# GLA gate logits of a hybrid encoder layer: both products first, ScalarE moves them out of PSUM, VectorE's clamp moves into a later instruction

## The chip, the cores and the metric

The kernel runs on one NeuronCore of a Trainium2 chip. The metric is the device time of one execution in microseconds (us). The core's engines work side by side, each through its own instruction list in order: TensorE (PE in the profile), VectorE (DVE), ScalarE (ACT), GpSimd (POOL) and SyncE (SP), which here only issues DMAs. They meet at semaphores: an instruction that needs another engine's result waits, and everything behind it on its engine waits too.

## What is computed

One layer of a streaming encoder over 2048 prompt tokens and 32 sample tokens, model width 1024. After an RMSNorm one projection feeds a sliding-window attention and a gated linear attention (GLA, 4 heads with 64-wide keys and 128-wide values). Both outputs go through `w_out`, then a feed-forward with squared ReLU. The change lies in GLA's forget gate:

```python
log_a = jax.nn.log_sigmoid((ca @ w_alpha + b_alpha)) / GLA_TAU      # 16 -> 256 columns, TAU = 16
def step(S, inp):                                                   # gla_chunked, one chunk
    qc, kc, vc, gc = inp
    b = jnp.cumsum(gc, axis=1)
    o_inter = jnp.einsum('blhk,bhkv->blhv', qc * jnp.exp(b), S)
    ... # o_intra: q.k products weighted with exp(b_t - b_s), causal, times v
    S_new = jnp.exp(bL)[..., None] * S + jnp.einsum('bshk,bshv->bhkv', kc * jnp.exp(bL - b), vc)
```

The kernel computes `log_sigmoid(x)` as `min(x, 0) - ln(1 + exp(-|x|))`, and its running sum over the tokens of a 128-token tile.

## The kernel before

The program has three phases: attention (to about 395 us), GLA with the start of `w_out` (to about 810 us), and the feed-forward, which fills the rest with dense matmuls. Matrix products split each fp32 operand into a high and a low part and add three products.

The GLA phase goes through eight pairs of token tiles, called halves 0 to 7 in the code (half 0 also has the 32 sample tokens). For each half `project` computes q (`zq`, two products), k (`zk`, two) and v (`zv`, one for each tile). VectorE scales q and k out of PSUM into the tile `kq` (L721). For each token tile a generator `gla_tile` then runs these steps:

- GpSimd forms differences of `cc`, the running sum of the log gate (tiles `E`, L790 and L798); ScalarE takes Abs and Exp of them (L800, L113); VectorE multiplies them with k and q (L805, L809).
- TensorE computes the blocks `A` of the token-by-token matrix (104 small matmuls, into two PSUM tiles A0 and A1). VectorE copies them with masks into the buffer AT (L863, L869, L874), and the diagonal from `dk` (L821). TensorE transposes the decayed keys into `dk`; ScalarE moves them to `kdT`.
- TensorE computes the outputs `go` and the state update; VectorE updates the state `Sp` (L906); ScalarE squares `go` (into the second half of the tile `v`, L912); VectorE sums the squares (`ssg`, L913), takes an inverse root by small instructions (L170 to L175), and scales into `g` (L918). Later TensorE transposes `g` (`gTp`), ScalarE copies it (`gT`, L927), and SyncE stores it.

The forget gate of the next half is computed by the generator `decay`. It loads `ca`, multiplies it with `wal` (two products of 128 columns, the tile name `la`), and from that makes `la` and `cc`. In halves 1 to 7 both products lie in one PSUM tile, `one_bank`. With each product ScalarE takes the absolute value with the bias (L649), and VectorE takes the clamped value with the bias (L650). Then ScalarE takes Exp and Ln (L113, each with a table load before it), VectorE subtracts (L655) and takes the running sum by two scans (L657). `tail` is `gates`, which applies Silu to the output gate tiles `g` on ScalarE; GpSimd then multiplies them with a constant (L702).

The order of TensorE's list is fixed by the order in which the Python code issues matmuls. The order on the other engines is set by the scheduler of the tile framework, which works with its own estimates and with priorities. The framework adds the waits: a matmul that writes to a PSUM tile waits for the earlier readers of that tile, and two engines that read one PSUM tile do so one after the other. The PSUM pool `pss` has five tiles, which `la`, `dk`, `A0`, `A1`, `gTp` and `go` share; `psm` has three, for `zq`, `zk` and `zv`.

Of the kernel before, what the change touches and what calls it, by code (L numbers as in the profile page):

```python
# [12 lines left out]
AF = mybir.ActivationFunctionType  # L13
ALU = mybir.AluOpType
# [5 lines left out]
P = 128  # L20
# [8 lines left out]
class Builder:  # L29
# [600 lines left out]
    def decay(self, h, tail=None):  # L630

        V, S, Q = self.V, self.S, self.Q
        _, d0, wal, bal, one, _ = self.gla_consts
        tiles = self.halves[h]
        N = sum(self.rows(t) for t in tiles)
        resets = d0 if h == 0 else d0[:, NS:]
        tmp = self.io_tile(f"la_{h}")
        la, ca = tmp[:, :576].rearrange("p (q t) -> p q t", q=2), tmp[:16, 576:864]
        off = 0
        for t in tiles:  # L640
            Q.dma_start(ca[:, off : off + self.rows(t)], self.cad[t])
            off += self.rows(t)
        yield 5000 + 4000 * (h == 0)
        cc = self.cc[h] = self.mid.tile([P, 2, 288], F32, tag="cc", name=f"cc_{h}")
        one_bank = N <= 2 * P and self.ps_s(f"la_{h}")
        for p in range(2):
            ps = one_bank[:, p * N : (p + 1) * N] if one_bank else self.ps_s(f"la_{h}_{p}")[:, :N]
            self.mm(ps, wal[:, p * P : (p + 1) * P], ca[:, :N], True, True)
            S.activation(la[:, p, :N], ps, AF.Abs, bias=bal[:, p : p + 1])  # L649
            V.tensor_scalar(out=cc[:, p, :N], in0=ps, scalar1=bal[:, p : p + 1], scalar2=0.0, op0=ALU.add, op1=ALU.min)  # L650
        self.table(la[:, :, :N], la[:, :, :N], AF.Exp, scale=-1.0)
        self.table(la[:, :, :N], la[:, :, :N], AF.Ln, bias=one)
        if tail:
            tail(h)
        V.tensor_tensor(out=la[:, :, :N], in0=cc[:, :, :N], in1=la[:, :, :N], op=ALU.subtract)  # L655
        for p in range(2):
            V.tensor_tensor_scan(  # L657
                out=cc[:, p, :N], data0=resets, data1=la[:, p, :N], initial=0.0, op0=ALU.mult, op1=ALU.add
            )

    def gla_phase(self):
        tc, a, V, S, G, Q = self.tc, self.a, self.V, self.S, self.G, self.Q
        nt = self.nt
        with ExitStack() as ctx:
# [3 lines left out]
            masks, d0, wal, bal, one, ones = self.gla_consts  # L668
# [16 lines left out]
            vs, gs, vready, glas, stage, decs = {}, {}, set(), [], {}, {0: self.dec0}  # L685

            def reach(n, s):

                while n >= 0 and stage[n] < s:
                    self.clock = max(self.clock, glas[n][0])  # L690
                    self._resume(glas[n])
# [12 lines left out]
            def project(h):  # L704
                tiles = halves[h]
                (nh, nl), N, rb = self.gla_toks.pop(h)
                rh, rl = (lambda kb: nh[:, kb, :N]), (lambda kb: nl[:, kb, :N])

                kq = wk.tile([P, 4 * 288], F32, tag="kq", name=f"kq_{h}")
                offs = np.cumsum([0] + [self.rows(t) for t in tiles])  # L710
                runs = [(0, 1, NS)] * (len(tiles) == 3) + [(N - 2 * P, 2, P)]
                for wt, x, sc, nm in ((self.wqg, 1, 0.125, "q"), (self.wkg, 0, 1.0, "k")):
                    for p in range(2):
                        if h == 0 and self.head0:
                            ps = self.head0.pop(0)
                        else:
                            ps = self.gla_cols(wt, p, f"z{nm}_{h}_{p}", rh, rl, N)
                        for at, j, L in runs:
                            dst = kq[:, 4 * at : 4 * (at + j * L)].rearrange("q (j x p t) -> q x p j t", j=j, x=2, p=2)[:, x, p]
                            src, rbs = (y[:, at : at + j * L].rearrange("q (j t) -> q j t", j=j) for y in (ps, rb))  # L720
                            V.scalar_tensor_tensor(out=dst, in0=src, scalar=sc, in1=rbs, op0=ALU.mult, op1=ALU.mult)  # L721
                wvg = self.wvg
                if h == len(halves) - 1:
                    self.prepare_ffn(1)
                    self.prepare_ffn(0)
                self.finish(decs[h])
                for i, t in enumerate(tiles):
                    r = self.rows(t)
                    if i < 2:
                        n = len(glas)  # L730
                        reach(n - 2, 2)
                        glas.append(None)
                        glas[n] = self.spawn(gla_tile(n, t, int(offs[i]), kq, self.cc[h]), 0 if i else 0)
                        self.tick()
                    ts = slice(int(offs[i]), int(offs[i]) + r)
                    ps = self.ps_m(f"zv_{t}")[:r]
                    self.gemm_wide(ps, lambda kb: nh[:, kb, ts], lambda kb: nl[:, kb, ts], wvg)
                    reach(len(vs) - 3, 3)
                    vs[t] = self.io_tile(f"v_{t}")
                    S.activation(vs[t][:r, :512], ps, AF.Copy, scale=self.rstd[:r, t : t + 1])  # L740
                    vready.add(t)
                    if h == len(halves) - 1 and i == len(tiles) - 1:
                        self.prepare_ffn(2)
                    if i == 2:
                        n = len(glas)
                        reach(n - 2, 2)
                        glas.append(None)
                        glas[n] = self.spawn(gla_tile(n, t, int(offs[i]), kq, self.cc[h]), 0)
                        self.tick()
                    if i == len(tiles) - 2 and h + 1 < len(halves):  # L750
                        decs[h + 1] = self.spawn(self.decay(h + 1, gates), 1500)
# [13 lines left out]
            def gla_tile(n, t, off, kq, cc):  # L765
                stage[n] = 0
                L = self.rows(t)
# [3 lines left out]
                kq, cv = kq[:, 4 * off : 4 * (off + L)].rearrange("q (x p t) -> q x p t", x=2, p=2), cc[:, :, tk]  # L771
                k, q = kq[:, 0], kq[:, 1]
# [1 line left out]
                NL = len(lv)  # L774
                first = key == "p" and t == 0
                qk = wk.tile([P, 2, P], F32, tag="qkp", name=f"qkp_{t}")
                (G if 0 else V).tensor_tensor(out=qk[:, :, :L], in0=q, in1=k, op=ALU.mult)
                ec = wk.tile([P, 2, P], F32, tag="ec", name=f"ec_{t}", bufs=3)
                self.table(ec[:, :, :L], cv, AF.Exp, scale=1.0 / 16)
                if not first:  # L780
                    Qc = wk.tile([P, 2, P], F32, tag="Qc", name=f"Qc_{t}", bufs=3)
                    (G if 0 else V).tensor_tensor(out=Qc[:, :, :L], in0=q, in1=ec[:, :, :L], op=ALU.mult)
                Es = []
                for gi, g_ in enumerate([list(range(0, 4)), list(range(4, NL + 1))]):
                    E = wk.tile([P, 4, 2 * P], F32, tag="E", name=f"E_{t}_{gi}", bufs=4)
                    E = E[:, :, : 2 * L].rearrange("q s (p t) -> q s p t", p=2)
                    for s_, li in enumerate(g_):
                        ev = E[:, s_]
                        if li == NL:
                            G.tensor_tensor(  # L790
                                out=ev, in0=cv[:, :, L - 1 : L].broadcast_to([P, 2, L]), in1=cv, op=ALU.subtract
# [23 lines left out]
                ps = self.ps_s(f"dk_{t}")  # L815
# [12 lines left out]
                def K(li):  # L828
                    return Es[0][:, li] if li < 4 else Es[1][:, li - 4]
# [12 lines left out]
                for li, m in enumerate(lv):  # L842
# [3 lines left out]
                    for p in range(2):  # L846
                        for a0 in range(nh if m < 64 else 1):
                            s0, s1 = (slice(0, 64), slice(64, P)) if m == 64 else (slice(a0 * 64, a0 * 64 + L // nh),) * 2
                            for hh in range(2):
                                x = K(li)[hh * 64 : hh * 64 + 64, p]  # L850
# [8 lines left out]
                for li, m in enumerate(lv):  # L859
                    for hh in range(2):  # L860
                        src = at[li][hh]
# [3 lines left out]
                        for a0 in range(nh):  # L865
# [6 lines left out]
                            dst = A4[r, :, hh, r].rearrange("s p (n h m) -> s p n h m", h=2, m=m)[:, :, :, 1, :]  # L872
# [15 lines left out]
                ps = [self.ps_s(f"go{hh}_{t}") for hh in range(2)]  # L888
# [525 lines left out]
```

## Time and profile before

| | us |
|---|---|
| three runs | 2373.58, 2368.15, 2366.94 (median 2368.15) |
| the profiled execution | 2377.03 (span 2375.2) |
| TensorE busy in the span | 2270.3 |
| VectorE busy | 1454.0 |
| GpSimd busy | 1161.2 |
| ScalarE busy | 950.0 |

Times in rows are counted from the first instruction of the span. A row of the timeline gives start, duration, engine, line, operation, output and inputs, how many instructions are merged in it, and in brackets how long the engine was idle before it and what ended that. A row of the waits gives total, number and longest. A row of the windows gives, for a stretch, its length, the busy time and number of instructions of PE, PEld (weight loads), DVE, ACT and POOL, then the granted TensorE clock as a share of full speed, and the DMA share and rate. In the chain of work that ended last, a row gives start, duration and what worked.

### The profile page before, as it was taken

Reading aid. Unit: us, or ns where it says so; the run is one execution under the profiler, and the core shown is the slowest. Engines: PE = TensorE matmul, PEld = TensorE weight load, DVE = VectorE, ACT = ScalarE, POOL = GpSimd, SP = SyncE. Lnnn points to the kernel's source line nnn. Section 1 sums busy time; section 2 is a strip of 40 time slices with the busy share of each in tenths; the row PEclk is TensorE's granted clock in tenths of the full one; section 3 lists DMA queues with packets and bytes.
Section 4 is the critical chain, followed back from the end, with each engine's and each line's share of the span. In section 5 each row is a group of like instructions: output and inputs, shape, how many; then the busy total and the mean of one; then the engine's idle time right before and its main releaser. Section 6 shows DMA issues by size and latency. Waiting matters only on the chain.

```text
span 2375.2 us, 39804 instructions
## 1 busy us (share of the span) xinstructions
PE 2270.3 (96%) x15389; PEld 2128.0 (90%) x15389; DVE 1454.0 (61%) x3686; ACT 950.0 (40%) x1945; POOL 1161.2 (49%) x956
## 2 busy tenths in 40 slices
PE   6999999899887899999999899999999999999999
PEld 5777776688776899999999899999999999999999
DVE  6666656688778755555564755555556655555555
ACT  3554444454452633333334533333334533333331
POOL 3221224232241457766754466666663546666662
PEclk8999999889898999999999999999999999999999
DMA  8864564322322422232226222222227122222211
GB/s 205 157 127 101 129 164 121 85 73 59 101 82 74 120 80 72 77 102 72 71 84 194 80 72 71 72 71 72 72 61 222 36 80 72 72 71 72 72 63 51
DMA packets 214461, 221.56 MB, mean 93 GB/s; under 512 B 38736, under 2 KB 178976, under 8 KB 214272
## 3 DMA queue, kind: packets, MB, share of 16 engines
q1 hardware_dynamic: 214272, 219.02, 32.9%
q8 instruction: 121, 1.98, 0.3%
q14 instruction: 68, 0.56, 0.1%
HBM read 180.08 MB, written 38.91 MB: 92 GB/s over the span
## 4 chain that ended last, share of the span: by engine, by line
PE 85%; DVE 8%; DMA 3%; ACT 1%; POOL 1%; issue 1%; SPq 0%; ACTq 0%; DVEq 0%; POOLq 0%
PE dn L105 30%; PE op L105 7%; PE zq L105 5%; PE PS4B L105 4%; PE PA11B L105 4%; PE PA12B L105 4%; PE PS2T L105 3%; PE PS1T L105 3%; PE PA22T L105 3%; PE PS3T L105 3%; PE zr L105 3%; PE zv L105 3%; PE zkv L105 2%; PE go L105 2%; PE zk L105 2%; PE O L105 1%
## 5 line engine op out<-in xcount | busy, mean ns | idle before, releaser
L1082 POOL TENSOR_TENSOR wu<-stage,wu 128x512 fp32r<-128x512 f32 x336 | 435.4, 1305 | 525.0 <-ACT wu L1081 525.0
L1249 DVE TENSOR_TENSOR y<-y,dn 128x360 f32<-128x360 f32 (+1 forms) x768 | 392.6, 515 | 219.6 <-PE dn L105 216.7
L1081 ACT ACTIVATE wu<-stage 128x512 fp32r<-128x512 f32 x336 | 206.0, 627 | 488.6 <-PE dn L105 224.7
L1084 POOL TENSOR_TENSOR stage<-stage 128x512 f32<-128x512 f32 x192 | 250.7, 1306 | 7.5
L1202 ACT ACTIVATE r<-PA11B 128x360 f32<-128x360 f32 (+1 forms) x48 | 22.1, 460 | 315.6 <-PE PA11B L105 315.6
L1189 DVE TENSOR_TENSOR PA12B<-PA12B,r 128x360 f32<-128x360 f32 (+1 forms) x48 | 25.3, 527 | 150.2 <-PE PA12B L105 150.2
L702 POOL TENSOR_TENSOR g<-g,ggla 128x512 f32<-128x512 f32 (+1 forms) x17 | 22.2, 1330 | 194.2 <-ACT g L113 194.2
L105 PE MATMUL PS2T<-T2h,wu 128*128 128x360 f32 (+1 forms) x384 | 100.5, 324 | 13.4 <-ACT T2h L1114 13.4
L105 PE MATMUL PA22T<-T4h,wu 128*128 128x360 f32 (+1 forms) x384 | 102.7, 331 | 0.0
L105 PE MATMUL PS4B<-B22h,wu 128*128 128x360 f32 (+1 forms) x384 | 101.5, 328 | 0.0
L105 PE MATMUL PS3T<-T3h,wu 128*128 128x360 f32 (+1 forms) x384 | 99.7, 323 | 0.0
L105 PE MATMUL PS1T<-T1h,wu 128*128 128x360 f32 (+1 forms) x384 | 98.8, 321 | 0.0
L105 PE MATMUL PA11B<-B11h,wu 128*128 128x360 f32 (+1 forms) x384 | 98.8, 321 | 0.0
L105 PE MATMUL PA12B<-B21h,wu 128*128 128x360 f32 (+1 forms) x384 | 98.7, 321 | 0.0
L874 DVE COPY_PREDICATED AT<-masks,A 64x64 f32<-64x64 int32 (+1 forms) x330 | 82.8, 253 | 13.4 <-PE A L105 3.5
L105 PEld LDWEIGHTS PS2T<-T2h,wu 128*128 128x128 f32 x384 | 68.8, 190 | 14.2 <-ACT T2h L1114 14.2
L798 POOL TENSOR_TENSOR E<-cc 128x256 f32<-128x256 f32 (+1 forms) x117 | 68.3, 619 | 17.8 <-PE A L105 17.8
L497 ACT ACTIVATE P<-S,negm 128x192 f32<-128x192 f32 (+2 forms) x128 | 51.6, 417 | 51.7 <-DVE negm L492 34.9
L105 PEld LDWEIGHTS PA22T<-T4h,wu 128*128 128x128 f32 x384 | 71.2, 196 | 0.0
L105 PEld LDWEIGHTS PS4B<-B22h,wu 128*128 128x128 f32 x384 | 70.1, 193 | 0.0
L105 PEld LDWEIGHTS PS3T<-T3h,wu 128*128 128x128 f32 x384 | 69.1, 190 | 0.0
L105 PEld LDWEIGHTS PS1T<-T1h,wu 128*128 128x128 f32 x384 | 68.1, 188 | 0.0
(1006 smaller groups left out, 7766.4 us busy)
## 6 DMA issues: line engine op xcount, KB each, us to landing
stage<-in_w_up SPq DMA_DIRECT2D x96, 512.0 KB, 3.8
stage<-in_w_down SPq DMA_DIRECT2D x96, 512.0 KB, 3.8
stage<-in_w_out SPq DMA_DIRECT2D x24, 512.0 KB, 4.7
xT1a<-in_xT_prompt SPq DMA_DIRECT2D x16, 512.0 KB, 8.8
stage<-in_w_in SPq DMA_DIRECT2D x16, 512.0 KB, 5.0
x1a<-in_x_prompt SPq DMA_DIRECT2D x16, 512.0 KB, 6.6
out_yT_prompt<-y SPq DMA_DIRECT2D x32, 180.0 KB, 3.0
m<-mixT SPq DMA_DIRECT2D x11, 512.0 KB, 3.9
```

The costliest lines, as they stand in the source:

```text
L105: self._pe(self.T.matmul(out, lhsT, rhs, start=start, stop=stop), ns)
L497: S.activation(Pt[:, u, :n], sp[:, jp], AF.Exp, bias=negm[:, ch, u : u + 1], scale=0.125, accum_out=rsum[:, ch, u : u + 1],)
L702: G.tensor_tensor(out=gv, in0=gv, in1=ggla[:r].unsqueeze(1).broadcast_to([r, 4, P]), op=ALU.mult)
L798: G.tensor_tensor(out=e4, in0=c4, in1=ref, op=ALU.subtract)
L874: V.copy_predicated(dst, mk.unsqueeze(1).broadcast_to([L // nh, 2, w // m, m]), src[r].rearrange("s p (n m) -> s p n m", m=m),)
L1081: S.activation(h, src, AF.Copy)
L1082: G.tensor_tensor(out=l, in0=src, in1=f32(h), op=ALU.subtract)
L1084: tt = lambda o, x, y, op: G.tensor_tensor(out=o, in0=x, in1=y, op=op)
L1189: tt = lambda out, x, y, op=ALU.add: V.tensor_tensor(out=out, in0=x, in1=y, op=op)
L1202: S.activation(r0, product(b, "A11", "B11"), AF.Copy)
L1249: V.tensor_tensor(out=yg[:, f, :], in0=yg[:, f, :], in1=ps, op=ALU.add)
```

## The change

In `decay` both matmuls are issued before anything reads them. ScalarE then moves each product out with its bias (Identity, into `cc`), and takes the absolute value of both at once from `cc` in SBUF. VectorE no longer reads the PSUM tile. Its clamp `min(x, 0)` becomes the first operation of the subtraction, now a scalar_tensor_tensor. In `project` the scaling of q and k gets a higher scheduling priority. Two other edits of the diff (a choice that was always VectorE, a delay that was always 0) change nothing.

```diff
@@ decay @@
-        one_bank = N <= 2 * P and self.ps_s(f"la_{h}")
+        if N <= 2 * P:
+            x = self.ps_s(f"la_{h}")
+            ps = [x[:, p * N : (p + 1) * N] for p in range(2)]
+        else:
+            ps = [self.ps_s(f"la_{h}_{p}")[:, :N] for p in range(2)]
         for p in range(2):
-            ps = one_bank[:, p * N : (p + 1) * N] if one_bank else self.ps_s(f"la_{h}_{p}")[:, :N]
-            self.mm(ps, wal[:, p * P : (p + 1) * P], ca[:, :N], True, True)
-            S.activation(la[:, p, :N], ps, AF.Abs, bias=bal[:, p : p + 1])
-            V.tensor_scalar(out=cc[:, p, :N], in0=ps, scalar1=bal[:, p : p + 1], scalar2=0.0, op0=ALU.add, op1=ALU.min)
+            self.mm(ps[p], wal[:, p * P : (p + 1) * P], ca[:, :N], True, True)
+        for p in range(2):
+            S.activation(cc[:, p, :N], ps[p], AF.Identity, bias=bal[:, p : p + 1])
+        S.activation(la[:, :, :N], cc[:, :, :N], AF.Abs)
         self.table(la[:, :, :N], la[:, :, :N], AF.Exp, scale=-1.0)
         self.table(la[:, :, :N], la[:, :, :N], AF.Ln, bias=one)
         if tail:
             tail(h)
-        V.tensor_tensor(out=la[:, :, :N], in0=cc[:, :, :N], in1=la[:, :, :N], op=ALU.subtract)
+        V.scalar_tensor_tensor(
+            out=la[:, :, :N], in0=cc[:, :, :N], scalar=0.0, in1=la[:, :, :N], op0=ALU.min, op1=ALU.subtract
+        )
@@ project @@
-                            V.scalar_tensor_tensor(out=dst, in0=src, scalar=sc, in1=rbs, op0=ALU.mult, op1=ALU.mult)
+                            with tc.high_priority(500):
+                                V.scalar_tensor_tensor(out=dst, in0=src, scalar=sc, in1=rbs, op0=ALU.mult, op1=ALU.mult)
```

The lists of TensorE and GpSimd keep their order, instruction for instruction. SyncE's list differs at one place (one load of `w_out` now stands behind the load of `g_15` and the store of `gT_10`). VectorE's and ScalarE's lists change around each `decay`. Half 3 stands for halves 3 to 6; numbers at the end of a name tell buffers apart.

VectorE, half 3, from the last masked copies of A of token tile 4 to the first use of the new `cc`; before:

```order
L874 COPY_PREDICATED AT1_4493<-masks_2828,A0_4_5856 64x2x32 x2
L874 COPY_PREDICATED AT1_4493<-masks_2828,A1_4_5857 64x2x32 x2
L650 TENSOR_SCALAR cc_3_5936<-la_3_5937,packed_177 128x256
L821 COPY_PREDICATED AT0_4492<-packed_177,dk_5_5965 128x512
L655 TENSOR_TENSOR la_3_5803<-cc_3_5936,la_3_5803 128x2x256
L657 SCALAR_TENSOR_TENSOR cc_3_5936<-d0_2829,la_3_5803 128x256 x2
L721 SCALAR_TENSOR_TENSOR kq_3_5838<-zq_3_0_5839,rb_3_5265 128x2x128
L721 SCALAR_TENSOR_TENSOR kq_3_5838<-zq_3_1_5984,rb_3_5265 128x2x128
L782 TENSOR_TENSOR Qc_6_6196<-kq_3_5838,ec_6_6194 128x256
```

and in the changed kernel:

```order
L881 COPY_PREDICATED AT1_4492<-masks_2828,A0_4_5853 64x2x32 x2
L881 COPY_PREDICATED AT1_4492<-masks_2828,A1_4_5854 64x2x32 x2
L659 SCALAR_TENSOR_TENSOR la_3_5800<-cc_3_5933,la_3_5800 128x2x256
L728 SCALAR_TENSOR_TENSOR kq_3_5835<-zq_3_0_5836,rb_3_5263 128x2x128
L663 SCALAR_TENSOR_TENSOR cc_3_5933<-d0_2829,la_3_5800 128x256 x2
L728 SCALAR_TENSOR_TENSOR kq_3_5835<-zq_3_1_5980,rb_3_5263 128x2x128
L789 TENSOR_TENSOR Qc_6_6192<-kq_3_5835,ec_6_6190 128x256
```

The two clamps are gone (the other stood among the masked copies of A), the copy from `dk_5` has moved in among the masked copies, and the first scaling of q has moved ahead of the scans.

ScalarE, half 3, from the move of `kdT_4` to Silu of the gate tiles; before:

```order
L836 ACTIVATE kdT_4_5854<-dk_4_5806 128x256
L649 ACTIVATE la_3_5803<-la_3_5937,packed_177 128x256 x2
L113 ACTIVATE la_3_5803<-la_3_5803 128x2x256
L927 ACTIVATE gT_2_5955<-gTp_2_5950 128x512
L113 ACT_TABLE_LOAD
L113 ACTIVATE la_3_5803<-la_3_5803,one_2831 128x2x256
L113 ACT_TABLE_LOAD
L113 ACTIVATE g_6_5946<-g_6_5946 128x512
```

and in the changed kernel:

```order
L843 ACTIVATE kdT_4_5851<-dk_4_5803 128x256
L653 ACTIVATE cc_3_5933<-la_3_5934,packed_177 128x256 x2
L934 ACTIVATE gT_2_5951<-gTp_2_5946 128x512
L654 ACTIVATE la_3_5800<-cc_3_5933 128x2x256
L113 ACTIVATE la_3_5800<-la_3_5800 128x2x256
L113 ACT_TABLE_LOAD
L113 ACTIVATE la_3_5800<-la_3_5800,one_2831 128x2x256
L113 ACT_TABLE_LOAD
L113 ACTIVATE g_6_5942<-g_6_5942 128x512
```

There is one Abs of 512 columns more, and the copy `gT_2` now stands ahead of Abs and Exp. The number of table loads is the same.

ScalarE, half 7, around the squares of token tile 12; before:

```order
L800 ACTIVATE E_15_0_8400<-E_15_0_8400 128x1024
L912 ACTIVATE v_12_7843<-go0_12_8192 128x256
L800 ACTIVATE E_15_1_8411<-E_15_1_8411 128x1024
L912 ACTIVATE v_12_7843<-go1_12_8193 128x256
L113 ACTIVATE ec_15_8396<-cc_7_8007 128x256
```

and in the changed kernel:

```order
L807 ACTIVATE E_15_0_8392<-E_15_0_8392 128x1024
L919 ACTIVATE v_12_7836<-go0_12_8184 128x256
L919 ACTIVATE v_12_7836<-go1_12_8185 128x256
L113 ACTIVATE ec_15_8388<-cc_7_8000 128x256
L113 ACTIVATE E_15_0_8392<-E_15_0_8392 128x1024
```

Abs of `E_15_1` no longer stands between the two squares; its Exp has moved behind two casts of `w_out` weights.

More of the change, by code (lines that the diff above doesn't have):

```diff
@@ L732, in project @@
                         glas.append(None)
-                        glas[n] = self.spawn(gla_tile(n, t, int(offs[i]), kq, self.cc[h]), 0 if i else 0)
+                        glas[n] = self.spawn(gla_tile(n, t, int(offs[i]), kq, self.cc[h]))
                         self.tick()
@@ L776, in gla_tile @@
                 qk = wk.tile([P, 2, P], F32, tag="qkp", name=f"qkp_{t}")
-                (G if 0 else V).tensor_tensor(out=qk[:, :, :L], in0=q, in1=k, op=ALU.mult)
+                V.tensor_tensor(out=qk[:, :, :L], in0=q, in1=k, op=ALU.mult)
                 ec = wk.tile([P, 2, P], F32, tag="ec", name=f"ec_{t}", bufs=3)
@@ L781, in gla_tile @@
                     Qc = wk.tile([P, 2, P], F32, tag="Qc", name=f"Qc_{t}", bufs=3)
-                    (G if 0 else V).tensor_tensor(out=Qc[:, :, :L], in0=q, in1=ec[:, :, :L], op=ALU.mult)
+                    V.tensor_tensor(out=Qc[:, :, :L], in0=q, in1=ec[:, :, :L], op=ALU.mult)
                 Es = []
```

## Prediction

> **What bounds the kernel now.** I read the page's engine shares first, then TensorE's waits, then the stretches of the GLA phase, then the rows of one half there.
>
> ```profile
> PE 2270.3 (96%) x15389; PEld 2128.0 (90%) x15389; DVE 1454.0 (61%) x3686; ACT 950.0 (40%) x1945; POOL 1161.2 (49%) x956
> PE la L105 <- DVE cc L650: 20.9, 7, 6.0
> 513.50:555.44 41.94, 39.55 (x439) 33.27 (x433) 34.15 (x121) 20.16 (x29) 12.45 (x18) 0.92 0.30 82
> 517.00:520.00 3.00, 3.00 (x18) 2.10 (x17) 2.69 (x11) 2.28 (x4) 0.00 (x0) 0.50 0.79 173
> 720.00:760.00 40.00, 26.71 (x343) 23.22 (x342) 37.31 (x105) 9.77 (x17) 6.69 (x3) 0.90 0.33 100
> ```
>
> TensorE bounds the program as a whole, so what it stops waiting for is the first thing to count. Its largest wait of all is the one this change takes away: 20.9 us in seven places, the second `la` product of halves 1 to 7 behind VectorE's clamp of the first. The third row is one half, 41.94 us from the `la` of half 3 to that of half 4. VectorE is busy there for 34.15 us, and that leaves out the short pauses between its instructions, so it is close behind TensorE. The last row is the end of the GLA phase, where VectorE is busy 37.31 us of 40 and TensorE 26.71.
>
> ```profile
> 513.52 0.69 PE L105 MATMUL la<-la,wal 16*128 16x256 f32 x2
> 516.61 1.02 PE L105 MATMUL la<-la,wal 16*128 16x256 f32 x2 [2.39 <-DVE cc L650]
> 513.65 0.48 DVE L863 COPY AT<-A 64x128 f32<-64x128 f32 x2 [2.42 <-PE A L105]
> 516.07 0.48 DVE L650 TENSOR_SCALAR cc<-la,packed 128x256 f32<-128x256 f32 x1
> 521.13 0.49 DVE L650 TENSOR_SCALAR cc<-la,packed 128x256 f32<-128x256 f32 x1
> 521.54 0.73 DVE L821 COPY_PREDICATED AT<-packed,dk 128x512 f32<-128x512 int32 x1
> 522.16 0.68 DVE L655 TENSOR_TENSOR la<-cc,la 128x512 f32<-128x512 f32 x1
> 522.87 2.33 DVE L657 TENSOR_TENSOR_SCAN cc<-d,la 128x256 f32<-128x256 f32 x2
> 523.37 2.92 POOL L702 TENSOR_TENSOR g<-g,ggla 128x512 f32<-128x512 f32 x2 [33.02 <-ACT g L113]
> 519.20 6.46 PE zq L105 x36
> 533.08 4.43 PE zk L105 x36
> 517.63 1.04 PE gTp L109 x4
> 527.40 0.59 PE gTp L109 x4
> ```
>
> The first clamp starts at 516.07, behind copies of A, and TensorE stands still for 2.39 us. Right behind that the granted clock is 0.50 (517 to 520 above). 36 matmuls of zq take 6.46 us there, and 36 of zk, of the same shape, 4.43 us at full clock; four transposes take 1.04 against 0.59. With 0.33 on the second `la` (1.02 against 0.69) the slow stretch costs 2.8 us.
>
> **TensorE's side.** Without the wait a half costs TensorE 41.94 - 2.39 - 2.8 = 36.7 us. Over seven halves that is 20.9 + 7 x 2.8 = 40.5 us, if TensorE then waits for nothing else. The Trainium skill ("TensorE: Matmul & The Clock Gate", section "Why this matters for your kernels") says the clock falls after idle gaps of more than about 3 us. The trace differs: it fell behind 2.39 us. By the page's figure only the 20.9 us would come.
>
> **VectorE's side decides.** The same half on VectorE, GpSimd and ScalarE:
>
> ```profile
> 526.25 3.21 POOL L798 TENSOR_TENSOR E<-cc 128x256 f32<-128x256 f32 x5
> 529.11 0.28 DVE L863 COPY AT<-A 64x128 f32<-64x128 f32 x1 [2.46 <-PE A L105]
> 535.21 0.61 POOL L790 TENSOR_TENSOR E<-cc 128x256 f32<-128x256 f32 x1
> 535.85 1.06 ACT L800 ACTIVATE E<-E 128x1024 f32<-128x1024 f32 x1 [1.20 <-POOL E L790]
> 537.49 0.69 DVE L913 TENSOR_REDUCE ssg<-v 128x4 f32<-128x512 f32 x1 [0.64 <-ACT v L912]
> 555.57 0.48 DVE L863 COPY AT<-A 64x128 f32<-64x128 f32 x2 [2.21 <-PE A L105]
> 564.76 1.27 DVE L657 TENSOR_TENSOR_SCAN cc<-d,la 128x256 f32<-128x256 f32 x2
> ```
>
> VectorE waits for TensorE's A twice in a half (2.42 and 2.46; 2.21 at the next). With TensorE 5 us ahead those waits close, and a loop is left that does not pass through TensorE: scans, GpSimd's E, ScalarE's Abs and squares, `ssg`, the products of E, the copies of A, the scans again. Step by step:
> - End of the scans to the end of GpSimd's E: 526.25 to 535.82 is 9.6 us, and 0.1 ahead of it.
> - To `ssg` at 537.49: 1.7 us (Abs 1.06 and the squares queued behind it).
> - `ssg` to the point where VectorE is ready for the next A: 555.57 - 2.21 - 537.49 = 15.9 us.
> - The copies of A, 513.65 to 521.13, less the one clamp between them: 7.0 us.
> - L821 to the subtraction 0.6, the subtraction 0.7, the scaling of zq that now comes ahead of the scans 0.4.
> - The scans: 1.27 us by themselves (half 4), 2.33 where GpSimd's L702 ran beside them (half 3).
>
> The sum is 37.3 us with free scans and 38.3 with the slow ones. I take 38.3: without the wait ScalarE's Silu, and with it L702, moves about 2 us ahead of VectorE's copies, so L702 will run beside the subtraction or the scans in every half. The Trainium skill ("SBUF — State Buffer", section "SBUF: two separate sides") says that an instruction of VectorE with two SBUF inputs and one of GpSimd that reads SBUF exclude each other for their whole length. The 2.33 agrees; by that rule the subtraction can lose as much, and the loop would be 39.4, and the sum below 4.4 us less.
>
> So a half goes from 41.94 to 38.3: 3.6 us, not the 5.2 of TensorE. Four steps from half to half (3 to 7) give 4 x 3.6 = 14.4 us.
>
> **The edits by themselves.** Per half ScalarE loses two Abs with bias, gains two Identity of the same shape and one Abs of 512 columns. VectorE loses two clamps and has scalar_tensor_tensor for tensor_tensor.
>
> ```profile
> L649 ACT ACTIVATE la<-la,packed x16: 457/474/538, 387.7 to 688.9; 128x256 f32<-128x256 f32 x14, 128x288 f32<-128x288 f32 x2
> L113 ACT ACTIVATE la<-la x8: 621/631/687, 388.6 to 689.4; 128x512 f32<-128x512 f32 x7, 128x576 f32<-128x576 f32 x1
> L650 DVE TENSOR_SCALAR cc<-la,packed x16: 469/484/512, 388.4 to 691.8; 128x256 f32<-128x256 f32 x14, 128x288 f32<-128x288 f32 x2
> 425.34 0.69 DVE L655 TENSOR_TENSOR la<-cc,la 128x512 f32<-128x512 f32 x1 [1.86 <-ACT la L113]
> 476.57 0.69 DVE L655 TENSOR_TENSOR la<-cc,la 128x512 f32<-128x512 f32 x1 [2.25 <-ACT la L113]
> ```
>
> Identity has no row; I price it as the Abs that it replaces, 0.47, with 0.63 (the 512-column form) as the other end. The new Abs is 0.63 by the Exp of that shape. The two clamps were 2 x 0.48 us; in the loop one of them is out of the copies, the other out of the 0.4 us in front of L821. The new subtraction lies between 0 and 0.1 us longer (it reads the same bytes as the 0.69 us of L655).
>
> ScalarE has room in halves 3 to 7, since there VectorE comes to the subtraction without a wait. In halves 1 and 2 it does not: VectorE stands 1.86 and 2.25 us for Ln. There Abs (0.63), and in ScalarE's new order also a `kdT` and a `gT`, stand ahead of Ln, while the wait of TensorE saves 2.2 and 1.1 us that nothing bound by VectorE can use. I count a loss of 0.7 us for both, between +1 and -2.
>
> **Half 7 and the end.**
>
> ```profile
> 687.63 1.22 PE L105 MATMUL la<-la,wal 16*128 16x256 f32 x2 [6.00 <-DVE cc L650]
> 685.97 0.40 ACT L960 ACTIVATE m0h<-m 128x256 fp32r<-128x256 f32 x1
> 688.88 0.47 ACT L649 ACTIVATE la<-la,packed 128x256 f32<-128x256 f32 x1 [2.51 <-PE la L105]
> 709.09 1.06 ACT L800 ACTIVATE E<-E 128x1024 f32<-128x1024 f32 x1 [3.61 <-POOL E L798]
> 711.37 1.06 ACT L800 ACTIVATE E<-E 128x1024 f32<-128x1024 f32 x1 [0.96 <-POOL E L790]
> 712.74 0.69 DVE L913 TENSOR_REDUCE ssg<-v 128x4 f32<-128x512 f32 x1 [5.26 <-ACT v L912]
> ```
>
> ScalarE's second read of `la` waits for TensorE to 688.88. Now both reads follow the casts of m (the last row of those ends at 686.4), so the chain starts 2.5 us earlier, less 0.6 for Abs: 1.9. At 712.74 VectorE has waited 5.26 us for a square that stands behind Abs of `E_15_1` (711.37). In the new order it follows Abs of `E_15_0` and ends near 709.09 + 1.06 + 2 x 0.38 = 710.9 instead of 712.7: 1.8 more. From there to 760 VectorE is the bound and shifts as a whole.
>
> **Sum.** -0.7 + 14.4 + 1.9 + 1.8 = 17.4 us. The feed-forward is not touched and starts that much earlier. The profiled execution took 2377.0 us, so it would take 2359.6; the median of the runs is 8.9 below that execution, and less 17.4 it is 2350.8, which I round to 2351.
>
> **Rivals.** A change within 0.3% (7.1 us) can hardly be told from none.
> - TensorE gets all it lost: 40.5 us, 2328. For it: the copies of A wait for TensorE in every half. Against: the loop of 38.3 us, and the end phase. It holds if VectorE's copies are not late for TensorE's next `go` before the last half.
> - Given back at the end: 720 to 760 may not move with VectorE but hang on loads of m and `w_out` weights, or stalls of 2 us return in each half (TensorE waits at `go` for AT, and the clock falls again). Then a half gains 1 to 2 us and the sum is 3 to 9; 2359 to 2365.
> - Only the waits go and the slow clock stays, since A, `la`, `gTp` and `dk` are small matmuls in a row: 2.4 to 3.4 us a half, about the same sum, 2353.
> - Slower: ScalarE becomes the bound of the gate in every half. Ahead of Ln it now has Abs (0.63), `gT` (0.60) and at times `kdT` (0.37), 1.6 us; if VectorE waits for Ln in all seven halves as in halves 1 and 2 and nothing else moves, that is 11 us, 2379. It decides once VectorE reaches the subtraction before Ln; in half 3 it came right behind L821, with no wait.
> - The change does nothing (a wait for the first `la` remains and takes all): TensorE's second product has no wait of its own in the new list, so this needs the wait to reappear at `gTp`. Counted with the second.
>
> **How the numbers follow.** The VectorE loop, with or without the slow clock: 0.6, from 2342 to 2356 (half by half 3 to 5 us). TensorE in full, or most of it: 0.14. Given back: 0.2, about half of it above 2361. Slower: 0.06. Faster by over 0.3% means below 2361: 0.6 + 0.14 + 0.11 = 0.85; within it 0.11; slower 0.04. The range takes in the ends of the first three: 2330 to 2362.
>
> **What the profile of the changed kernel would show.** The wait of PE `la` for `cc` is gone, and no granted clock of 0.50 follows `la` in halves 3 to 6. From one `la` to the next there are about 38 us. VectorE's waits for A in those halves fall below 1 us, a wait of `ssg` for the squares of 2 to 3 us takes their place, and scans of 2.3 us appear beside L702. `ssg` of token tile 12 waits less than 4 us. Clearly wrong I would be if halves stay at 41 us, with TensorE waiting at `go` or `gTp`, or if they fall to 36.

## The result, and the profile after

The changed kernel takes 2356.3 us (median of 4 runs, 2354.8 to 2357.9) against 2370.9 (4 runs, 2366.9 to 2374.1) of the kernel before on the same chip: ratio 0.9937, 95% interval 0.9924 to 0.9949, that is 14.6 us faster (12 to 18). The forecast was 17.4 us faster, 2351. The profiled execution took 2357.7 us (span 2355.9).

The first line of the page, and TensorE's waits (total, times, longest), of the kernel after:

```profile
PE 2271.3 (96%) x15389; PEld 2130.4 (90%) x15389; DVE 1452.7 (62%) x3670; ACT 953.4 (40%) x1953; POOL 1163.2 (49%) x956
```

```profile
PE dk L109 <- DVE AT L828: 6.0, 3, 3.3
PE go L105 <- ACT kdT L843: 4.5, 3, 1.6
PE la L105 <- issue: 1.2, 2, 0.6
```

The busy times are those of before within 3.4 us each. VectorE has 16 instructions fewer (the clamps), but is busy only 1.3 us less, since its subtractions and scans take longer now (rows below). The wait of `la` for `cc`, 20.9 us, is gone. The waits of `dk` for AT and of `go` for `kdT` are new: in the kernel before, TensorE waited nowhere at `dk` for AT, and at most 0.6 us in all at `go` for `kdT` (L843 is L836 of before).

The half from the `la` of half 2 and the four up to that of half 7, from the windows of the kernel after (length, then busy time and count of PE, PEld, DVE, ACT, POOL, then granted clock, DMA share, GB/s):

```profile
466.54:510.16 43.62, 43.28 (x541) 37.30 (x539) 36.54 (x138) 21.57 (x32) 12.30 (x18) 0.86 0.19 53
510.16:550.93 40.77, 39.41 (x439) 33.29 (x433) 33.87 (x119) 20.76 (x30) 12.44 (x18) 0.92 0.30 84
550.93:589.41 38.48, 36.50 (x438) 30.86 (x433) 33.76 (x119) 20.89 (x30) 12.45 (x18) 1.00 0.35 98
589.41:627.85 38.44, 37.33 (x432) 31.97 (x433) 33.84 (x120) 20.78 (x30) 12.45 (x18) 0.96 0.30 87
627.85:666.38 38.53, 38.53 (x432) 33.18 (x432) 33.97 (x121) 22.14 (x32) 12.62 (x18) 0.91 0.30 86
```

Three of the last four take 38.44 to 38.53 us, whether the clock is 0.91 or 1.00 and whether TensorE is busy for 36.50 or for all 38.53 of it. A length that does not follow TensorE's load or clock is set elsewhere. Half 3 to 4, 40.77, is the exception.

The instructions at the end of the gate in half 5, from the timeline, and behind them ScalarE's Identity from the list of the instructions of `la` (minimum, median, maximum in ns):

```profile
597.11 2.96 POOL L708 TENSOR_TENSOR g<-g,ggla 128x512 f32<-128x512 f32 x2 [24.73 <-ACT g L113]
597.21 1.72 DVE L659 SCALAR_TENSOR_TENSOR la<-cc,la 128x512 f32<-128x512 f32 x1
599.31 1.89 DVE L663 TENSOR_TENSOR_SCAN cc<-d,la 128x256 f32<-128x256 f32 x2
612.49 0.69 DVE L920 TENSOR_REDUCE ssg<-v 128x4 f32<-128x512 f32 x1 [2.23 <-ACT v L919]
```

```profile
L653 ACT ACTIVATE cc<-la,packed x16: 459/470/538, 384.8 to 671.7; 128x256 f32<-128x256 f32 x14, 128x288 f32<-128x288 f32 x2
```

GpSimd's L708 (L702 of before) now starts 0.1 us ahead of the subtraction. The subtraction takes 1.72 us and the scans 1.89. In half 6 L708 starts 0.3 us behind the start of the subtraction instead; there the subtraction takes 0.67 us and the scans 3.05.

For all profiles taken, the GLA phase in three stretches, in us, from the starts of the `la` products and of the last group of eight `go` products (with `v` and `kdT`):

| profile | `la` 0 to 3 | `la` 3 to 7 | `la` 7 to last `go` | sum |
|---|---|---|---|---|
| before, three profiles | 127.2, 126.9, 125.2 | 167.4, 167.4, 166.5 | 81.7, 79.7, 79.8 | 376.4, 374.0, 371.5 |
| after, two profiles | 127.2, 125.0 | 156.2, 154.4 | 77.2, 78.8 | 360.6, 358.2 |
| both products first only | 129.7 | 160.7 | 76.3 | 366.7 |
| without the priority, two | 127.0, 127.8 | 160.9, 160.8 | 75.9, 76.0 | 363.8, 364.6 |
| priority only | 127.2 | 167.3 | 76.8 | 371.3 |
| without g_gla | 127.2 | 152.8 | 76.9 | 356.8 |
| `kdT` ahead of `ec` | 127.7 | 154.4 | 76.6 | 358.7 |
| both of these | 125.6 | 153.8 | 78.9 | 358.2 |
| copies of A by ScalarE | 126.6 | 173.6 | 72.5 | 372.7 |
| scans twice | 132.9 | 160.9 | 77.9 | 371.7 |

By the means of the profiles the change gains 0.3 + 11.8 + 2.4 = 14.5 us, about what the timing says.

### The profile page after: what moved, and what is told of

It is laid out like the page before. It is cut to its first block, busy times and chain, and to the rows that moved or that the text cites. A ratio compares the mean times of both kernels' runs of the same rounds, so it can differ in the third digit from the quotient of the medians.

```text
span 2355.9 us, 39800 instructions
## 1 busy us (share of the span) xinstructions
PE 2271.3 (96%) x15389; PEld 2130.4 (90%) x15389; DVE 1452.7 (62%) x3670; ACT 953.4 (40%) x1953; POOL 1163.2 (49%) x956
## 4 chain that ended last, share of the span: by engine, by line
PE 79%; DVE 12%; DMA 3%; ACT 2%; POOL 2%; issue 1%; SPq 0%; DVEq 0%; POOLq 0%; ACTq 0%
PE dn L105 31%; PE op L105 7%; PE PS4B L105 4%; PE PA11B L105 4%; PE PA12B L105 4%; PE PS2T L105 4%; PE PS1T L105 3%; PE PS3T L105 3%; PE PA22T L105 3%; PE zq L105 3%; PE zr L105 3%; DVE AT L881 2%; PE zkv L105 2%; PE zv L105 2%; PE O L105 1%
## 5 line engine op out<-in xcount | busy, mean ns | idle before, releaser
L708 POOL TENSOR_TENSOR g<-g,ggla 128x512 f32<-128x512 f32 (+1 forms) x17 | 25.1, 1494 | 171.9 <-ACT g L113 171.9
```

The lines of the kernel that those rows point to most:

```text
L708: G.tensor_tensor(out=gv, in0=gv, in1=ggla[:r].unsqueeze(1).broadcast_to([r, 4, P]), op=ALU.mult)
```

## The experiments

**Both products first, and nothing else.**

```diff
+        ps = [one_bank[:, p * N : (p + 1) * N] if one_bank else self.ps_s(f"la_{h}_{p}")[:, :N] for p in range(2)]
         for p in range(2):
-            ps = one_bank[...] ...
-            self.mm(ps, wal[:, p * P : (p + 1) * P], ca[:, :N], True, True)
+            self.mm(ps[p], wal[:, p * P : (p + 1) * P], ca[:, :N], True, True)
+        for p in range(2):
             S.activation(la[:, p, :N], ps[p], AF.Abs, ...)
             V.tensor_scalar(out=cc[:, p, :N], in0=ps[p], ..., op1=ALU.min)
```

> The kernel before, with both la products issued first and nothing else: ScalarE's Abs and VectorE's clamps still read PSUM. Loop theory (the wait of TensorE goes with the order of the products, and then VectorE's loop of 38.4 us sets the half): the 20.9 us wait of la behind cc is gone; the two clamps stay on VectorE, 2 x 0.48 us a half in the loop, so a half takes about 39.4 us and the run is 10 to 12 us faster than before (ratio 0.995 to 0.996), short of the changed kernel's 14.6. Rival (what counts is that ScalarE takes the move out of PSUM, because the clamps hold the PSUM banks until VectorE comes to them): the wait only moves to gTp or the next product, under 4 us faster. Rival (TensorE is the bound of the half): the full 14.6 us.

Ratio 0.9972 (0.9963 to 0.9981), 6.6 us faster. Two of its halves, from its windows:

```profile
560.85:600.52 39.67, 36.69 (x439) 30.98 (x433) 33.17 (x121) 20.38 (x29) 12.30 (x18) 1.00 0.36 97
640.41:680.27 39.86, 38.31 (x432) 33.06 (x433) 33.02 (x122) 22.37 (x31) 11.95 (x18) 0.91 0.28 80
```

The wait of `la` is gone, and the halves of 39.7 to 39.9 us are near the 39.4 that the loop theory gave: TensorE has as little say in them as after. The whole gain is smaller than expected; halves 0 to 3 took 3.3 us more in this one profile (129.7 against 126.4 on average, where the kernel before spreads over 2 us). It is more than the under 4 us of the first rival and less than the 14.6 of the second. So the order of the products gives about half of the 14.6 us or less (4.5 to 8.8 by the interval). The rest is left for ScalarE's move with the clamp inside the subtraction, which takes the clamps out of VectorE's list, and for the priority; the next kernel divides these. In the halves from 4 to 7 (39.67 to 39.89 us here, 38.44 to 38.53 in the changed kernel) the rest is 1.3 us each.

**Without the priority on the scaling of q and k, twice; and the priority alone on the kernel before.**

```diff
-                            with tc.high_priority(500):
-                                V.scalar_tensor_tensor(out=dst, in0=src, scalar=sc, in1=rbs, ...)
+                            V.scalar_tensor_tensor(out=dst, in0=src, scalar=sc, in1=rbs, ...)
```

> The changed kernel without the priority on the scaling of q and k. Loop theory: the scaling is 0.4 us a piece and is wanted late, so its place is worth 0 to 2 us of the 14.6: ratio to before 0.994 to 0.995. Rival (the priority carries part of the gain): 4 us or more are lost, ratio above 0.9955.

> The changed kernel without the priority once more. Its first profile had one half of 43.2 us between halves of 38.5, with TensorE 2.8 us at go for kdT. Theory (chance: ec, which stands ahead of kdT on ScalarE, waits for the scans wherever VectorE happens to be late): no half above 41 us, or another one than 5 to 6. Rival (the order without the priority brings it): half 5 to 6 is again above 42 us.

> The kernel before with the priority on the scaling of q and k alone. Loop theory: the wait of la behind cc stays at about 21 us, and the time is within 3 us of before (ratio 0.9988 to 1.001). Rival (the priority carries part of the gain): 4 us or more faster, ratio below 0.9985.

Without the priority the ratio is 0.9952 (0.9938 to 0.9967), 11.4 us faster than before. That lies between the two expectations. It is 4.8 us more than with the order of the products alone, and about 3.5 us short of the changed kernel's 0.9937; in both comparisons the intervals overlap, so the division rests on the profiles. Both profiles show the same long half (the windows of the second):

```profile
555.72:594.21 38.49, 36.62 (x438) 30.86 (x433) 33.73 (x119) 20.89 (x30) 12.45 (x18) 1.00 0.35 98
594.21:637.36 43.15, 40.33 (x433) 34.45 (x433) 34.29 (x120) 20.87 (x30) 12.43 (x18) 0.88 0.23 66
637.36:675.82 38.46, 36.48 (x437) 30.77 (x433) 33.77 (x119) 22.79 (x32) 12.45 (x18) 1.00 0.32 99
```

It is not chance, then: the rival of the second run holds. ScalarE and TensorE in that half:

```profile
606.03 0.42 ACT L113 ACTIVATE ec<-cc 128x256 f32<-128x256 f32 x1 [2.38 <-DVE cc L663]
608.74 1.06 ACT L806 ACTIVATE E<-E 128x1024 f32<-128x1024 f32 x1 [2.29 <-POOL E L804]
609.70 0.37 ACT L842 ACTIVATE kdT<-dk 128x256 f32<-128x256 f32 x1
610.12 0.79 PE L105 MATMUL go<-Sp,Qc 64*128 64x128 f32 x2 [2.82 <-ACT kdT L842]
```

`kdT` stands behind Abs of E, which waits for GpSimd; TensorE's `go` waits 2.82 us for it and then runs at a low clock (0.88 over the half). ScalarE's list without the priority, and with it (numbers of the instructions left out):

```
 L ACTIVATE ec_10<-cc_5 128x256
+L ACTIVATE kdT_9<-dk_9 128x256
 L ACTIVATE E_10_0<-E_10_0 128x1024
-L ACTIVATE kdT_9<-dk_9 128x256
 L ACTIVATE E_10_0<-E_10_0 128x1024
```

Up to the tiles of half 7 that is the one difference between the two lists of ScalarE; TensorE's and GpSimd's lists are the same; VectorE's differ at several places. So the priority acts, and the wait that it spares TensorE hangs on the scheduler's order of another instruction on another engine. That this order alone makes the long half was not run by itself. On the kernel before the priority does nothing (1.0006, 0.9992 to 1.0020; the wait of `la` stays):

```profile
PE la L105 <- DVE cc L650: 21.4, 7, 6.0
```

In the kernel before, `kdT` stands behind Abs of E as well, in halves 3, 5 and 6 of all three profiles. Here is half 5 of the first:

```profile
612.60 1.06 ACT L800 ACTIVATE E<-E 128x1024 f32<-128x1024 f32 x1 [2.93 <-POOL E L798]
613.57 0.36 ACT L836 ACTIVATE kdT<-dk 128x256 f32<-128x256 f32 x1
```

TensorE hardly waits for it there: it has already lost 2.4 to 3.4 us at `la` in each of these halves. Where that wait is gone, a late `kdT` shows as a wait. In the changed kernel, and with both products first alone, it stands ahead of Abs of E in halves 3 to 6.

**The collision of GpSimd with VectorE.**

```diff
-                    G.tensor_tensor(out=gv, in0=gv, in1=ggla[:r].unsqueeze(1).broadcast_to([r, 4, P]), op=ALU.mult)
```

> The changed kernel without GpSimd's multiplication of g by g_gla (2 x 2.96 us a half are left out; the output lacks that scale). Loop theory with the collision: the subtraction falls from 1.72 to 0.7 us and the scans from 1.89 to 1.27 each, and halves 4 to 7 go from 38.5 to 36.7 to 37 us, where TensorE's own 36.7 takes over: 5 to 7 us below the changed kernel, ratio to before 0.991 to 0.992. Rival (TensorE or another chain already sets 38.5): the subtraction and scans are short but the halves stay at 38.4, ratio as the changed kernel's 0.994.

This kernel leaves out GpSimd's multiplication, so its output lacks that scale. By the rows of the changed kernel the multiplication takes 2.96 us for both instructions of a half together, and 1.89 us is the time of both scans, not of each as the expectation has it. Ratio 0.9936 (0.9924 to 0.9949): nothing gained over the changed kernel, where 5 to 7 us were expected. The collision is real, as VectorE's rows show:

```profile
597.14 0.69 DVE L659 SCALAR_TENSOR_TENSOR la<-cc,la 128x512 f32<-128x512 f32 x1
598.20 1.26 DVE L663 TENSOR_TENSOR_SCAN cc<-d,la 128x256 f32<-128x256 f32 x2
629.68 0.28 DVE L869 COPY AT<-A 64x128 f32<-64x128 f32 x1 [3.36 <-PE A L105]
```

```profile
513.49:550.72 37.23, 36.42 (x439) 30.86 (x433) 32.16 (x119) 20.73 (x30) 9.47 (x16) 1.00 0.36 99
550.72:589.26 38.54, 36.27 (x432) 30.78 (x432) 32.17 (x120) 20.77 (x30) 9.48 (x16) 1.00 0.28 79
589.26:629.54 40.28, 39.08 (x438) 33.41 (x432) 32.36 (x119) 20.79 (x30) 9.48 (x16) 0.92 0.29 83
629.54:666.29 36.75, 35.86 (x439) 30.52 (x433) 32.00 (x119) 22.30 (x32) 9.48 (x16) 1.00 0.36 102
```

The subtraction falls from 1.72 to 0.69 us and the scans from 1.89 to 1.26, 1.7 us in all, and two halves come down to 36.75 and 37.23, near the 36.7 of the forecast for TensorE alone. Which engine sets these two is not separated: TensorE is busy for 35.86 and 36.42 us of them, and VectorE's loop, 38.5 less 1.7, would also be 36.8. In the other two the scheduler has put `kdT` behind Abs of E, as in the long half above; TensorE waits 1.2 to 1.5 us at `go`, and VectorE then waits for TensorE (3.36 us for A at 629.68). Stretch 3 to 7 gains 2.5 us on the mean of the changed kernel, not 6; that is too little for the timing to show.

**The changed kernel again, and `kdT` ahead of `ec`.**

```diff
-                S.activation(kdT[:L], ps[:L, :256], AF.Copy)
+                self.last_kdT = S.activation(kdT[:L], ps[:L, :256], AF.Copy)
...
                 self.table(ec[:, :, :L], cv, AF.Exp, scale=1.0 / 16)
+                # order only: ec behind the kdT issued last
+                self.tc.add_manual_dep(self.last_table.ins, self.last_kdT.ins.name, NOSYNC, ...)
```

> The changed kernel once more, unaltered, for a second profile and as the yardstick on the chip of the next three. Ratio to before 0.993 to 0.995 again; halves 4 to 7 again 38.4 to 38.6 us where TensorE's clock stays up. Rival (the length of half 3 to 4, 40.8 us, and the place of the waits for kdT are chance): the same halves come out otherwise by over 1.5 us.

> The changed kernel with one order added on ScalarE: kdT of the tile before goes ahead of Exp of ec, which waits for the scans (0.36 us of work that stood ready 4 us behind that wait at 522.34). Theory (TensorE's wait at go for kdT, and the slow clock behind it, is what halves 1 to 4 lack of the forecast): the wait of go for kdT falls from 4.5 us below 1 us, half 3 to 4 falls from 40.8 to 38.5 us, and the run is 2 to 5 us below the changed kernel. Rival (VectorE's loop sets those halves all the same): the wait goes and the halves stay, within 1.5 us.

Again 0.9937 (0.9925 to 0.9949), and with `kdT` ahead 0.9945 (0.9933 to 0.9957): no gain. The first rows are windows of the changed kernel's second profile, the others of the kernel with `kdT` ahead:

```profile
467.51:509.85 42.34, 39.94 (x540) 34.02 (x538) 36.45 (x138) 21.49 (x32) 12.28 (x18) 0.96 0.22 62
509.85:548.67 38.82, 36.68 (x438) 30.90 (x433) 33.75 (x119) 20.67 (x30) 12.45 (x18) 1.00 0.35 96
548.67:587.26 38.59, 38.59 (x433) 33.00 (x433) 34.02 (x120) 20.90 (x30) 12.39 (x18) 0.91 0.28 78
```

```profile
472.49:516.12 43.63, 43.06 (x541) 37.08 (x539) 36.56 (x138) 21.20 (x32) 12.30 (x18) 0.87 0.15 46
516.12:554.94 38.82, 37.68 (x438) 32.10 (x433) 33.76 (x119) 20.73 (x30) 12.45 (x18) 0.96 0.35 98
554.94:593.52 38.58, 38.58 (x432) 33.04 (x432) 34.31 (x120) 20.99 (x30) 12.46 (x18) 0.91 0.27 76
```

With the same lists half 3 to 4 took 40.77 us in one execution and 38.82 in the other, so the lists do not fix that length. In the execution with 40.77 the half before had run at a clock of 0.86, in the other at 0.96; the kernel without the priority, with `kdT` at the same place here, has 40.8 and 40.7. With `kdT` ahead it is 38.82 after a half at 0.87. So the order may save 2 us in some executions, but the timing shows no gain, and in the other halves the rival holds: the wait for `kdT` is gone and they stay at 38.5. My theory that this wait is what the forecast lacked is not borne out.

**Both together.** The order of the last experiment in the kernel without g_gla.

> The kernel without GpSimd's multiplication by g_gla (left out: g_gla's scale of the output), with kdT ahead of ec as well. Without the multiplication alone the halves from 3 to 7 took 37.2, 38.5, 40.3 and 36.8 us. Theory (the collision of GpSimd with VectorE and the wait for kdT are the two things that keep a half above TensorE's own 36.7): all four take 36.6 to 37.4 us and the run is 4 to 7 us below the one without the multiplication alone. Rival (the two longer halves have another cause): they stay above 38 in two of four.

Ratio 0.9931 (0.9918 to 0.9943). The halves took 37.21, 39.77, 39.98 and 36.80 us: two stay above 38, as the rival has it. In both of them the scheduler put Abs of E ahead of `kdT`, and the order that I added then holds `ec` behind both. ScalarE and VectorE in the second of them:

```profile
601.80 1.06 ACT L808 ACTIVATE E<-E 128x1024 f32<-128x1024 f32 x1 [4.51 <-POOL E L806]
602.76 0.36 ACT L844 ACTIVATE kdT<-dk 128x256 f32<-128x256 f32 x1
603.14 1.28 ACT L113 ACT_TABLE_LOAD   x1
604.44 0.42 ACT L113 ACTIVATE ec<-cc 128x256 f32<-128x256 f32 x1
```

```profile
604.89 0.59 DVE L790 TENSOR_TENSOR Qc<-kq,ec 128x256 f32<-128x256 f32 x1 [5.35 <-ACT ec L113]
```

VectorE stands 5.35 us for `ec`. In these two halves the experiment did not do what it was made for, so whether the two causes are all stays open there. The other two halves are near 36.7 again. In all the long halves without the collision (38.5 and 40.3, 39.8 and 40.0) `kdT` stands behind Abs of E.

**The unmasked copies of A by ScalarE.**

```diff
-                            V.tensor_copy(A4[:64, :, hh, 64:], src[:64])
+                            S.activation(A4[:64, :, hh, 64:], src[:64], AF.Copy)
...
-                                V.tensor_copy(A4[r1, :, hh, r2], src[r1])
+                                S.activation(A4[r1, :, hh, r2], src[r1], AF.Copy)
```

> The changed kernel with the twelve unmasked copies of A of a half done by ScalarE instead of VectorE (about 2.8 us a half off VectorE). Loop theory: VectorE's loop falls from 38.4 to under 36.7 us and TensorE sets the half, 36.7 to 37.5 us where its clock stays up: 3 to 6 us below the changed kernel. Rival (ScalarE's queue becomes the one that is late, with kdT and the squares behind the copies): TensorE waits for kdT in most halves, the clock falls, and the run is as the changed kernel or slower.

Ratio 1.0003 (0.9992 to 1.0013): the whole gain is lost. From VectorE's timeline and the windows:

```profile
571.62 2.54 DVE L881 COPY_PREDICATED AT<-masks,A 64x64 f32<-64x64 int32 x10 [7.38 <-ACT AT L876]
```

```profile
553.01:597.63 44.62, 39.63 (x433) 33.45 (x433) 31.31 (x108) 22.77 (x40) 12.68 (x18) 0.89 0.24 67
```

VectorE has 2.5 us less to do and the half is 6 us longer. ScalarE's copies stand behind two Abs and two Exp of E, which wait for GpSimd, and VectorE waits 7.38 us for them. The loop theory counted busy time and not the place in the queue; the rival holds, though what TensorE then waits for most is not `kdT` but the state `Sp`:

```profile
PE go L105 <- DVE Sp L913: 22.4, 7, 5.0
```

**The scans twice.**

```diff
-        for p in range(2):
+        for p in (0, 1, 0, 1):
             V.tensor_tensor_scan(
```

> The changed kernel with the two scans of each half done twice over (the second pair writes the same values), that is 1.27 us alone, or 1.9 us beside GpSimd, more on VectorE in the place that the loop passes through. Loop theory: halves 4 to 7 go from 38.5 to between 39.8 and 40.4 us each, and the run is 5 to 9 us above the changed kernel (ratio to before 0.9960 to 0.9975). Rival (TensorE, or a wait on ScalarE, sets 38.5 and VectorE has room): the halves stay within 0.5 us and the ratio within 0.9930 to 0.9945.

Ratio 0.9996 (0.9984 to 1.0007). A row of the timeline and the last halves:

```profile
648.88 3.19 DVE L663 TENSOR_TENSOR_SCAN cc<-d,la 128x256 f32<-128x256 f32 x4
```

```profile
559.82:599.46 39.64, 36.62 (x438) 30.85 (x433) 34.92 (x121) 20.89 (x30) 12.44 (x18) 1.00 0.34 94
599.46:639.10 39.64, 37.80 (x433) 32.09 (x433) 35.02 (x122) 20.90 (x30) 12.90 (x18) 0.96 0.30 85
639.10:678.78 39.68, 38.31 (x433) 33.07 (x433) 35.11 (x122) 22.51 (x32) 12.48 (x18) 0.91 0.29 84
```

The scans take 3.19 us instead of 1.89 (in half 5, where the subtraction takes 0.69, they take 4.09), and each half is 1.15 us longer (39.65 against 38.5), at three different clocks. This shows directly that a loop through VectorE's scans sets the half: TensorE, with 36.62 us of work in the first of these, has no say. The run lost more than expected (about 14 us against the changed kernel, not 5 to 9), since the three halves ahead of `la` 3 lost 6.7 us: there 1.3 us of VectorE cost 2.2. Why stays open.

**The kernel before, twice more.**

> The kernel before, unaltered, for a second profile. Theory (the stretch from the la of half 7 to the last go, 81.7 us in the first profile, is the 6.0 us wait of la and the late square): again 80 to 82 us, against 76 to 79 in the changed kernel. Rival (it is chance, since the kernel with the priority alone took 76.8 there with the wait still in it): 76 to 79 us.

> The kernel before once more, for the same question; and half 3 to half 7 again 165 to 169 us, against 154.4 to 156.2 in the two profiles of the changed kernel.

From `la` 7 to the last `go`: 79.7 and 79.8 us, after 81.7, just below the 80 to 82 of the theory; from half 3 to 7 167.4 and 166.5, as expected. The spread over the whole stretch is 2 us within one kernel, and the kernel with the priority alone had 76.8 there with its `la` wait intact. The spread lies in the later part: up to `ssg` of token tile 12 the kernel before takes 31.74 to 31.88 us from `la` 7, and the changed one 29.08 and 29.22. So 2.6 us are gained there, clear of the spread; behind it nothing can be told (47.9 to 49.9 us before, 48.1 and 49.5 after).

## Why the prediction was right, and where it missed

- **TensorE's wait goes, TensorE's side does not decide.** Right. The 20.9 us are gone and 14.6 came back, and halves of 38.5 us stand over TensorE's 36.5 to 38.5 of work.
- **The slow clock hangs on the wait.** Wrong as the only cause. The forecast that no half clock follows `la` in halves 3 to 6 failed: in the changed kernel the granted clock is 0.50 from 591.3 to 594.6 and from 628.8 to 635.5 us, behind the `la` of halves 5 and 6, and no wait of TensorE around these is over 0.6 us. It became rarer all the same (1.00 over half 4, where all four halves of before have 0.92 or less). With `kdT` ahead TensorE waits nowhere over 0.62 us around the `la` of half 4, and still (windows, then timeline of that kernel):

```profile
552.00:555.20 3.20, 2.42 (x107) 2.20 (x108) 2.86 (x16) 0.38 (x1) 0.00 (x0) 1.00 1.14 311
555.20:562.60 7.40, 7.40 (x39) 6.39 (x39) 6.65 (x27) 5.96 (x9) 0.00 (x0) 0.54 0.80 215
```

```profile
552.26 0.41 PE L109 MATMUL dk<-packed,E 128*128 128x128 f32 x2 [0.62 <-DVE rsq_y_g L171]
552.60 1.82 PE L105 MATMUL A<-E 64*64 64x64 f32 x104
554.94 1.36 PE L105 MATMUL la<-la,wal 16*128 16x256 f32 x4 [0.52 <-issue]
```

  The third rival had this part: the slow clock stays where A, `la`, `gTp` and `dk`, small matmuls in a row, follow each other. It cost nothing in the end, because VectorE's loop is longer by as much. The Trainium skill ("TensorE: Matmul & The Clock Gate", section "What's actually happening") has the clock halve after an idle window of about 3.4 us. The trace differs here: no gap ahead of 555.2 was over 0.62 us.
- **The loop of 38.3 us decides.** Right, and shown: 38.4 to 38.6 from half 4 to 7 in both profiles and with `kdT` ahead, 39.65 with 1.3 us added to the scans. The term 4 x 3.6 = 14.4 came out as 11.8. Of the 2.6, 2.1 are halves longer than 38.3 (38.8 on the mean of both profiles, with the 40.77 of half 3 to 4), and 0.6 is that I took 41.94 for each half of before, where the mean of three profiles is 41.78. Step by step, from half 5 to half 6 of the changed kernel: end of the scans to `ssg` 11.3 us (forecast 11.4); `ssg` to the next A 15.4 (15.9); from there to the subtraction 7.7 (7.6); subtraction to the end of the scans 4.0 (3.4).
- **L702 beside the scans only.** Mis-sized. It runs beside the subtraction as well, or beside the scans for longer, and costs 1.03 + 0.63 = 1.7 us a half, not 1.06. The way from `ssg` to the next A is shorter by about as much, so that 38.3 came out nearly right is in part luck; why that way is shorter stays open. The Trainium skill's rule that these two kinds of instruction exclude each other ("SBUF — State Buffer", section "SBUF: two separate sides") agrees with 0.69 and 1.72 us for the same subtraction: the second L708 starts at 598.35, when the first is done, and the subtraction ends 0.58 us behind that. The loop of 39.4 us that the prediction works out by that rule was 0.9 too long.
- **The edits.** Identity takes 0.47 us as priced, and the subtraction with the clamp 0.69 without GpSimd beside it. What was missed here is the priority: it was priced as the place of a 0.4 us instruction, and half 5 to 6 is 4.7 us longer without it, in both profiles, with `kdT` behind Abs of E. The sum does not suffer by it, since the changed kernel has `kdT` ahead.
- **Halves 1 and 2, -0.7.** Not separable: 0.3 better by the means, with a spread of 2 us in one kernel.
- **Half 7 and the end, 3.7.** 2.4 by the means of the whole stretch, 2.6 up to `ssg` of token tile 12. The square came as priced: from the start of Abs of E to that of `ssg` it takes 1.6 us, where it took 3.65. The kernel with the priority alone has this step too (1.6). The other step is mis-sized: Ln ends 1.8 us earlier in the half, as forecast, but VectorE comes to the subtraction only 0.3 to 0.6 us earlier, and GpSimd's two L708 then run beside the scans, which end 1.5 us later than before. In the kernel before GpSimd did this multiplication behind the scans and came to E 2.3 us after their end. So Abs of E starts 0.5 to 0.8 us earlier, not 1.9. And the sign that `ssg` of token tile 12 waits less than 4 us failed. It waits 4.36 us, 4.07 in the second profile, because Abs itself waits for GpSimd:

```profile
693.83 1.06 ACT L807 ACTIVATE E<-E 128x1024 f32<-128x1024 f32 x1 [4.39 <-POOL E L805]
695.47 0.69 DVE L920 TENSOR_REDUCE ssg<-v 128x4 f32<-128x512 f32 x1 [4.36 <-ACT v L919]
```

- **The rivals.** TensorE in full (2328) fell with the halves of 38.5 us. Given back (2359 to 2365): waits of 1.4 to 1.6 us at `go` for `kdT` did appear (up to 3.6 in the second profile), but with `kdT` ahead they are gone without a gain. Slower through ScalarE's chain of the gate: in the halves from 3 to 7 VectorE never waits for Ln. A ScalarE that is late is a real danger all the same, as the kernel with its copies of A shows; it came in at another place than the rival named.
- **The base.** The kernel before came out at 2370.9 in the comparison, not 2368.2. Of the 5.3 us between 2351 and 2356.3 that is 2.7, and the mis-sized terms are the rest (2.6 too much for halves 3 to 7, 1.3 for the end, and 1.0 too little ahead of half 3).
- **What VectorE waits for.** `ssg` waits for the squares 2.2 to 2.6 us in each of the four halves, as forecast. The waits for A (1.5, 1.9, 0, 0 us in the order of the halves) fell below 1 us in two of four only.

No version beat the changed kernel beyond what the timing can tell.

## What to carry to other kernels

When a wait of the busiest engine is taken away, work out the next loop that closes without that engine, instruction by instruction, and take the smaller of the two gains; a half that keeps its length at three different clocks is the sign that another engine sets it. Busy time alone does not tell whether work can be moved to an idle engine: where the new instruction stands in that engine's queue, and what the one ahead of it waits for, decides. Where a scheduler orders the lists, compare them on all engines after a change of priority, since the effect can be one instruction on an engine that the change does not name.

## What the runs showed of the hardware that was not expected

The granted clock fell to 0.50 with no wait of TensorE over 0.62 us ahead of it, behind 104 matmuls of 64x64 and the 16-row `la` (rows above, 0.54 over the whole window). And the same lists of instructions gave 40.77 and 38.82 us for the same half in two executions, where the half before had run at 0.86 and at 0.96.
